# Layer 0's low weight parts on GpSimd, and a half-length Fourier transform over positions, in a two-block fp32 network

## The chip, the cores and the metric

The kernel runs on one core of a Trainium2 chip, as one launch. The metric is the device time of a launch in microseconds (us), lower is better. Six engines work side by side, each on its own queue in order: TensorE (PE, matmuls; PEld are its weight loads), VectorE (DVE), ScalarE (ACT), GpSimd (POOL), SyncE (SP, which here only issues DMAs) and 16 DMA engines that all issuers share.

## The reference, cut to what matters

Two blocks of a network in float32, on 256 tokens of width 2048. The first block has two layers (index 0 and 1); layer 0 also carries 256 context tokens, so its projections have 512 tokens and layer 1's have 256. One layer:

```python
shift, scale, gate = split(silu(c) @ ada_w[l] + ada_b[l], 3)
h = rmsnorm(x, norm_g[l]) * (1 + scale) + shift
q, k, v, up, uf, g = split_proj(h @ w_in[l])
att = attention(rope(rmsnorm(q)), [kc; rope(rmsnorm(k))], [vc; v])
mixed = concat([att, multiscale_pool(up), fourier_mix(uf)])
x = x + gate * ((mixed * silu(g)) @ w_out[l])
```

`fourier_mix` takes, for each of 4 groups of 128 channels, the real part of a two-dimensional DFT over (256 positions, 128 channels), and then a linear map:

```python
uf = u.reshape(B, N, 4, 128)
f = jnp.fft.fft2(uf, axes=(1, 3), norm='ortho').real
y = jnp.einsum('bngc,gcd->bngd', f, fourier_w)
```

The second block (gated mixing, a linear recurrence, a feed-forward part with d_ff 6144) isn't touched by the change.

## The kernel before, in words

**Weight pages.** Every large projection streams its weights in pages of 128 x 1024 floats (512 KB). `_issue` (line 91) puts the load into SP's queue, into one of 5 `wraw` buffers. `_split` (line 104) makes two fp32r tiles of it: `whi`, the rounded page, on ACT (line 259, in `split`), and `wlo`, the rest `raw - whi`, on DVE (line 260). Both have 3 buffers. `mm3` (lines 203 to 205) then does three matmuls for each product: high x high, low x high (of the activations), high x low (of the weights). `execute` (line 111) keeps up to 3 pages split ahead of the step that uses them, so a page's split can start when the page three before it has been used by the matmuls.

**Order.** The program is a list of steps. A framework orders each engine's queue by priority and by when its own plan has an instruction ready; on the chip each queue then runs strictly in that order. From `end_startup` on (`self.hot`), the two instructions of a split get high priority.

**Layer 0.** Up to about 246 us the startup works off three quarters of layer 0's first projections while the first modulation is computed. Then `end_startup` runs, and to about 827 us follow the last quarter of the first projections, the attention, pooling and Fourier branches, the four gate groups, and the output projection (`w_out`), whose last 512 columns are done in two halves of 256 tokens (pages of 24 matmuls with 256 columns). In the trace, PE uses layer 1's pages from about 827 us on; there `begin_layer1` has run.

**The modulation of later stages.** Between the weight pages, `ada_span` (line 306) streams raw pages of `ada_w` through the same 5 `wraw` buffers, in one order with the weight pages. Each raw page of layer 0's stretch is worked off by four DVE instructions of 512 columns (line 324), alternately into an accumulator `acc[0]` in SBUF and `acc[1]` in PSUM. A `wraw` buffer comes free when its last reader is done.

**The branches.** Attention, pooling and Fourier are generators that `tick` interleaves with the main steps. `fourier_tail` (line 746) does, for each group and each 256 tokens, four fp32 matmuls over channels into a `misc` bank of PSUM (three such banks), a DVE copy to `z`, then four fp32 matmuls over positions with the 128 x 2 x 256 tables `cn` and `sn` (lines 759, 760) that sum into one bank `fy`, and an ACT copy into `mixed`. There are 8 such transforms in layer 0 (4 groups x 2) and 4 in layer 1. Each fp32 matmul of the program stands as two records in the trace.

**What else is on GpSimd.** The powers of the norms (line 493), the gains of context q and k (line 599), the windows of the pooling (line 727), the running sums of squares (line 907), and DMA issues for constants and for `reload` of `xT` (line 849).

Of the kernel before, what the change touches and what calls it, by code (L numbers as in the profile page):

```python
# [11 lines left out]
ALU = mybir.AluOpType  # L12
# [4 lines left out]
P = 128  # L17
# [11 lines left out]
def f(ap):  # L29
    return ap.bitcast(F32)  # L30


class Kern:
    def __init__(self, ctx, tc, a, out):
        self.tc, self.nc, self.a, self.out = tc, tc.nc, a, out
        self.pg = ctx.enter_context(tc.tile_pool(name="pg", bufs=1))
        self.ps = ctx.enter_context(tc.tile_pool(name="ps", bufs=1, space=PSUM))
        self.dr = ctx.enter_context(tc.tile_pool(name="dr", bufs=1, space=DRAM))
        self.q_slot = 0
        self.halves = {}  # L40
        self.queue, self.active = deque(), []
        self.slot, self.start_rate, self.start_acc, self.spent = 0, 0.5, 0.0, 0.0
        self.nacc = 0
        self.late = self.hot = False


    def A(self, name, dt=F32, shape=(P, 512)):
# [56 lines left out]
    def _split(self, raw, width):  # L104
        hi = self.pg.tile([P, 1024], F32R, tag="whi", bufs=3, name="whi")
        lo = self.pg.tile([P, 1024], F32R, tag="wlo", bufs=3, name="wlo")
        with self.tc.high_priority() if self.hot else nullcontext():
            self.split(hi[:, :width], lo[:, :width], raw[:, :width])
        return hi, lo

    def execute(self, steps, ahead=3):
# [456 lines left out]
        nc.vector.scalar_tensor_tensor(lo, y[:, :256], sh, f(hi), ALU.add, ALU.subtract)  # L568

    def end_startup(self):  # L570
        self.hot = True
        self.in_order.__exit__(None, None, None)

    def spill_x(self, ks):
# [171 lines left out]
    def fourier_tail(self, gi, u, n):  # L746
        nc = self.nc
        yield 2
        for i in range(n // 256):
            zp = self.misc("fz")  # L750
            for t in range(2):
                nc.tensor.matmul(zp[:, t * 256:(t + 1) * 256], u[:, (i * 2 + t) * P:(i * 2 + t + 1) * P],
                                 self.ab[gi // 2][:, gi % 2, :], start=True, stop=True)
            z = self.S("fzs", shape=(P, 2, 256))
            nc.vector.tensor_copy(z.rearrange("p a b -> p (a b)"), zp)
            yield 3
            y = self.misc("fy")
            for t in range(2):
                nc.tensor.matmul(y[:, :256], z[:, t, 0:P], self.cn[:, t, :], start=t == 0, stop=False)
                nc.tensor.matmul(y[:, :256], z[:, t, P:2 * P], self.sn[:, t, :], start=False, stop=t == 1)  # L760
            nc.scalar.copy(self.mixed(12 + gi)[:, i * 256:(i + 1) * 256], y[:, :256])
        self.npf += 1

    def gate(self, j, src, n):
# [157 lines left out]

    def begin_layer1(self):
        self.l = 1
        self.late = True
        self.qT = {}
        self.kv_alloc()
        self.mixed = lambda j: self.xT[j][:, 256:512]
        self.h = self.pr
# [507 lines left out]
```

## Time and profile before

| | us |
|---|---|
| median of 3 runs | 2365.49 (2364.34 to 2366.28) |
| the profiled execution | 2370.99 |
| its span, first to last instruction | 2369.3 |
| busy in the span: PE / DVE / ACT / POOL | 2273.9 / 1628.4 / 1007.0 / 211.3 |

The profiled execution is 5.5 us above the median, and 1.7 us of it lie around the span. "Busy" is the time an engine's instructions took; matmul ends are modelled and overlap, so the spacing of starts, not the duration of one, is what a matmul costs in a row of them. Starts are in us from the span's start.

### The profile page before, as it was taken

How to read it: one execution, taken by the hardware profiler on the slowest of the kernel's cores; microseconds unless marked ns; L12 is line 12 of the kernel's file. 1: busy time of each engine (PE TensorE's matmuls, PEld its weight loads, DVE VectorE, ACT ScalarE, POOL GpSimd, SP SyncE). 2: the span in 40 equal slices, each digit the busy share in tenths (PEclk: the TensorE clock that was granted, in tenths of full speed). 3: DMA queues.
4: the chain of work that ended last, by engine and by line, in shares of the span. 5: the costliest groups of instructions: out<-in, count | busy, mean ns of one | idle time of the engine just before them, and what ended most of it. 6: DMA issues, size and time to landing. Idle time of an engine off the chain costs nothing.

```text
span 2369.3 us, 37423 instructions
## 1 busy us (share of the span) xinstructions
PE 2273.9 (96%) x14672; PEld 1990.0 (84%) x14672; DVE 1628.4 (69%) x2603; ACT 1007.0 (43%) x1507; POOL 211.3 (9%) x262
## 2 busy tenths in 40 slices
PE   7999898999999899999999999999999999999998
PEld 3777576877777877889998799999999999988886
DVE  4345886989888878865687966766577667664444
ACT  3322233423222455434454654554455445543433
POOL 1000203010102110010040211210000000000100
PEclk9999899999999999999999999999999999999999
DMA  9865442556766657765454554566666666765554
GB/s 328 282 233 183 144 125 60 155 179 207 238 210 207 192 156 223 249 214 183 163 180 159 159 179 162 187 189 185 186 180 186 185 181 186 218 207 187 187 187 144
DMA packets 202721, 447.89 MB, mean 189 GB/s; under 512 B 15848, under 2 KB 60288, under 8 KB 202544
## 3 DMA queue, kind: packets, MB, share of 16 engines
q1 hardware_dynamic: 193088, 428.93, 57.7%
q0 software_dynamic: 3888, 11.18, 1.4%
q10 hardware_dynamic: 5568, 5.40, 0.8%
q8 instruction: 115, 1.88, 0.3%
q14 instruction: 62, 0.51, 0.1%
HBM read 437.05 MB, written 8.39 MB: 188 GB/s over the span
## 4 chain that ended last, share of the span: by engine, by line
PE 54%; DVE 5%; issue 2%; DMA 1%; ACT 1%; POOL 1%; POOLq 0%; ACTq 0%; DVEq 0%
PE acc L205 17%; PE acc L203 17%; PE acc L204 17%; DVE wlo L260 1%; DMA wraw<-in_ada_w_dram 1%; DVE acc L324 1%; ACT whi L259 0%; DMA gw_n<-in_gm_ws_dram 0%; DVE lr L1173 0%; POOL qrs L493 0%; DMA wraw<-in_w_in_dram 0%; DVE mx L684 0%; DVE h L1001 0%; PE sc L682 0%; PE rbc L522 0%
## 5 line engine op out<-in xcount | busy, mean ns | idle before, releaser
L260 DVE TENSOR_TENSOR wlo<-wraw,whi 128x1024 fp32r<-128x1024 f32 x608 | 749.3, 1236 | 503.9 <-ACT whi L259 498.6
L259 ACT CAST whi<-wraw 128x1024 fp32r<-128x1024 f32 x608 | 636.0, 1049 | 976.9 <-PE acc L204 478.7
L203 PE MATMUL acc<-phi,whi 128*128 128x256 f32 (+1 forms) x1600 | 484.6, 303 | 14.3 <-DVE th L769 5.4
L205 PE MATMUL acc<-phi,wlo 128*128 128x256 f32 (+1 forms) x1600 | 477.8, 299 | 5.7 <-DVE wlo L260 5.7
L204 PE MATMUL acc<-plo,whi 128*128 128x256 f32 (+1 forms) x1600 | 477.4, 298 | 0.0
L203 PE MATMUL acc<-h3t,whi 128*128 128x256 f32 x1536 | 434.3, 283 | 1.3 <-DVE xT L1259 1.3
L204 PE MATMUL acc<-h3t,whi 128*128 128x256 f32 x1536 | 433.9, 283 | 0.0
L205 PE MATMUL acc<-h3t,wlo 128*128 128x256 f32 x1536 | 433.8, 282 | 0.0
L203 PEld LDWEIGHTS acc<-phi,whi 128*128 128x128 f32 x1600 | 306.6, 192 | 31.9 <-issue 9.7
L205 PEld LDWEIGHTS acc<-phi,wlo 128*128 128x128 f32 x1600 | 306.1, 191 | 17.2 <-DVE wlo L260 7.5
L324 DVE SCALAR_TENSOR_TENSOR acc<-wraw,silu_c,acc 128x512 f32<-128x512 f32 x420 | 301.3, 756 | 20.0 <-DMA wraw<-in_ada_w_dram 18.5
L204 PEld LDWEIGHTS acc<-plo,whi 128*128 128x128 f32 x1600 | 306.8, 192 | 9.2 <-issue 0.7
L203 PEld LDWEIGHTS acc<-h3t,whi 128*128 128x128 f32 x1536 | 293.3, 191 | 1.7 <-DVE xT L1259 1.7
L205 PEld LDWEIGHTS acc<-h3t,wlo 128*128 128x128 f32 x1536 | 293.4, 191 | 0.2 <-DVE wlo L260 0.2
L204 PEld LDWEIGHTS acc<-h3t,whi 128*128 128x128 f32 x1536 | 293.4, 191 | 0.0
L203 PE MATMUL acc<-hhi,whi 128*128 128x512 f32 x384 | 162.6, 424 | 5.2 <-ACT whi L259 5.2
L205 PE MATMUL acc<-hhi,wlo 128*128 128x512 f32 x384 | 154.3, 406 | 2.8 <-DVE wlo L260 2.8
L204 PE MATMUL acc<-hlo,whi 128*128 128x512 f32 x384 | 155.3, 404 | 0.0
L204 PE MATMUL acc<-wlo,act 128*128 128x512 f32 x384 | 151.7, 395 | 0.0
L203 PE MATMUL acc<-whi,act 128*128 128x512 f32 x384 | 151.7, 395 | 0.0
L205 PE MATMUL acc<-whi,act 128*128 128x512 f32 x384 | 151.7, 395 | 0.0
L203 PEld LDWEIGHTS acc<-hhi,whi 128*128 128x128 f32 x384 | 73.4, 191 | 29.0 <-ACT whi L259 7.2
(354 smaller groups left out, 2823.7 us busy)
## 6 DMA issues: line engine op xcount, KB each, us to landing
wraw<-in_w_in_dram SPq DMA_DIRECT2D x216, 512.0 KB, 3.9
wraw<-in_ffn_w_up_dram SPq DMA_DIRECT2D x192, 512.0 KB, 3.6
wraw<-in_ada_w_dram SPq DMA_DIRECT2D x128, 512.0 KB, 4.4
wraw<-in_w_out_dram SPq DMA_DIRECT2D x104, 512.0 KB, 4.4
wraw<-in_ffn_w_down_dram SPq DMA_DIRECT2D x96, 512.0 KB, 4.5
apage<-in_ada_w_dram SPq DMA_DIRECT2D x128, 256.0 KB, 5.6
xd<-xT SPq DMA_DIRECT2D x16, 256.0 KB, 3.7
xT<-xd POOLq DMA_DIRECT2D x16, 256.0 KB, 5.3
```

The source lines that it names most:

```text
L203: mm(out, lhi, rhi, start=start, stop=False)
L204: mm(out, lhi, rlo, start=False, stop=False)
L205: mm(out, llo, rhi, start=False, stop=stop)
L259: self.nc.scalar.copy(hi, src)
L260: self.nc.vector.tensor_tensor(lo, src, f(hi), ALU.subtract)
L324: nc.vector.scalar_tensor_tensor(acc[m], x, cm, acc[m], ALU.mult, ALU.add)
```

## The change

Two edits. First, `wlo` of a weight page is computed by GpSimd instead of DVE for the pages that are split between `end_startup` and `begin_layer1`; the rounded part stays on ACT. Second, the transform over positions computes its cosine and sine parts for positions 0 to 128 only, in two column ranges of one bank; ACT copies the sine part to SBUF, and DVE writes the sum for positions 0 to 128 and the difference, read backwards, for positions 129 to 255.

```diff
@@ class Kern, __init__
-        self.late = self.hot = False
+        self.late = self.hot = self.wide = False
@@ _split
         with self.tc.high_priority() if self.hot else nullcontext():
-            self.split(hi[:, :width], lo[:, :width], raw[:, :width])
+            self.nc.scalar.copy(hi[:, :width], raw[:, :width])
+            eng = self.nc.gpsimd if self.wide else self.nc.vector
+            eng.tensor_tensor(lo[:, :width], raw[:, :width], f(hi[:, :width]), ALU.subtract)
@@ end_startup
-        self.hot = True
+        self.hot = self.wide = True
@@ fourier_tail
             y = self.misc("fy")
-            for t in range(2):
-                nc.tensor.matmul(y[:, :256], z[:, t, 0:P], self.cn[:, t, :], start=t == 0, stop=False)
-                nc.tensor.matmul(y[:, :256], z[:, t, P:2 * P], self.sn[:, t, :], start=False, stop=t == 1)
-            nc.scalar.copy(self.mixed(12 + gi)[:, i * 256:(i + 1) * 256], y[:, :256])
+            for x, (tab, o) in enumerate(((self.cn, 0), (self.sn, P))):
+                for t in range(2):
+                    nc.tensor.matmul(y[:, x * 256:x * 256 + 129], z[:, t, o:o + P], tab[:, t, 0:129], start=t == 0,
+                                     stop=t == 1)
+            q = z[:, 0, 0:129]
+            nc.scalar.copy(q, y[:, 256:385])
+            m = self.mixed(12 + gi)[:, i * 256:(i + 1) * 256]
+            nc.vector.tensor_tensor(m[:, 0:129], y[:, 0:129], q, ALU.add)
+            nc.vector.tensor_tensor(m[:, 129:256], y[:, 127:0:-1], q[:, 127:0:-1], ALU.subtract)
@@ begin_layer1
-        self.late = True
+        self.late, self.wide = True, False
```

## Rows read from the trace of the kernel before

**Rows 1.** By stage: us, busy us of PE, PEld, DVE, ACT, POOL, PEclk, DMA, GB/s

```profile
246.00:440.00 194.00, 175.67 (x825) 136.94 (x825) 156.81 (x323) 66.06 (x137) 36.82 (x56) 0.95 0.37 108
440.00:607.00 167.00, 165.85 (x787) 130.50 (x785) 148.19 (x249) 55.71 (x95) 12.70 (x25) 1.00 0.61 189
607.00:760.00 153.00, 142.58 (x612) 110.28 (x613) 132.75 (x201) 37.73 (x49) 16.80 (x17) 0.97 0.67 212
760.00:827.00 67.00, 59.06 (x433) 55.38 (x432) 55.31 (x88) 29.06 (x42) 10.52 (x9) 0.92 0.62 200
```

**Rows 2.** Waits of PE from 246 to 827 us: total, times, longest

```profile
PE acc L203 <- ACT whi L259: 9.0, 3, 5.2
PE pTp L694 <- DVE p L690: 6.3, 3, 3.4
PE acc L203 <- DVE th L769: 5.4, 2, 4.5
PE acc L205 <- DVE wlo L260: 4.3, 3, 2.8
PE acc L203 <- DVE xT L855: 3.5, 4, 1.4
```

**Rows 3.** Waits of SP's queue, the page loads, 246 to 827 us

```profile
SPq L101 <- DVE wlo L260: 180.0, 63, 21.7
SPq L101 <- DVE acc L324: 167.9, 81, 5.6
```

**Rows 4.** Groups by line, DVE, 246 to 827 us: busy, mean ns, idle before

```profile
L324 DVE SCALAR_TENSOR_TENSOR acc<-wraw,silu_c,acc 128x512 f32<-128x512 f32 x351 | 249.7, 756 | 5.4 <-DMA wraw<-in_ada_w_dram 4.5
L260 DVE TENSOR_TENSOR wlo<-wraw,whi 128x1024 fp32r<-128x1024 f32 x83 | 104.4, 1257 | 44.5 <-ACT whi L259 41.4 <-PE poolmm L737 1.8 <-PE acc L204 0.9
```

**Rows 5.** Chain that ended last, 985 to 1062 us: start, us, what

```profile
997.81 2.68 PE pv L700 x24
...
1037.72 1.73 PE fz L752 x8
...
1044.64 0.43 PE fy L759 x2
```

**Rows 6.** Tile fy: count, ns min/median/max, first and last start

```profile
L759 PE MATMUL fy<-cn,fzs x48: 377/379/379, 324.4 to 1058.7; 128*128 128x256 f32 x48
L761 ACT COPY mix<-fy x8: 372/372/373, 326.3 to 354.8; 128x256 f32<-128x256 f32 x8
```

**Rows 7.** By 20 us, around layer 0's Fourier branch, columns as in Rows 1

```profile
320.00:340.00 20.00, 20.00 (x95) 16.95 (x94) 19.59 (x46) 3.02 (x10) 4.09 (x9) 1.00 0.54 158
340.00:360.00 20.00, 19.65 (x89) 14.67 (x88) 9.94 (x20) 8.06 (x16) 0.00 (x0) 1.00 0.19 53
```

**Rows 8.** Tile mix: DVE copies out of PSUM, 128 columns

```profile
L702 DVE COPY mix<-pv x32: 270/290/292, 312.9 to 484.2; 128x128 f32<-128x128 f32 x32
```

**Rows 9.** Tiles sq and x2r: GpSimd's two-input instructions, 256 and 512 columns

```profile
L907 POOL TENSOR_TENSOR sq<-sq,sqt x45: 727/932/1721, 1180.0 to 1544.9; 128x256 f32<-128x256 f32 x45
L1347 POOL TENSOR_TENSOR x2r<-x2r,fg x6: 1290/1578/2272, 2225.2 to 2296.4; 128x512 f32<-128x512 f32 x6
```

**Rows 10.** Order of time, POOL and DVE at 283 us: start, us, instruction

```profile
283.30 1.64 POOL L599 TENSOR_TENSOR qq<-qq,gb_q 128x512 f32<-128x512 f32 x1 [0.87 <-DVE qq L597]
...
283.73 2.28 DVE L260 TENSOR_TENSOR wlo<-wraw,whi 128x1024 fp32r<-128x1024 f32 x1
```

**Rows 11.** Tile plo, DVE: beside GpSimd's sums (h) and without them (yn)

```profile
L260 DVE TENSOR_TENSOR plo<-h,phi x16: 409/948/961, 1180.4 to 1253.9; 128x256 fp32r<-128x256 f32 x16
L260 DVE TENSOR_TENSOR plo<-yn,phi x16: 416/418/421, 1404.2 to 1459.8; 128x256 fp32r<-128x256 f32 x16
```

**Rows 12.** Groups by line, POOL, 246 to 827 us

```profile
L493 POOL TENSOR_TENSOR qrs<-qrs,nhalf 128x4 f32<-128x4 f32 (+1 forms) x12 | 12.3, 1025 | 79.3 <-DVE qrs L492 79.3
```

**Rows 13.** Order of time, PE at 1037 us: matmuls of 256 columns in a row

```profile
1037.20 0.28 PE L203 MATMUL acc<-phi,whi 128*128 128x256 f32 x1
1037.32 0.28 PE L204 MATMUL acc<-plo,whi 128*128 128x256 f32 x1
```

## The prediction, made before the change was run

> **What bounds the kernel now.** I read the page's busy shares first: PE is busy in 2273.9 of 2369.3 us, so whatever is changed can only pay through the matmuls it removes or through the time in which PE stands still. Next came the table by stage. In the stretch that the first edit touches, 246 to 827 us, PE is idle for 18.3 + 1.2 + 10.4 + 7.9 = 37.8 of 581 us, and DVE is busy in 493.1 of them [rows 1]. The reader is to see two engines near their limit at once: PE first, DVE close behind. Then the waits of PE in this stretch. Those that name DVE are 6.3 (p), 5.4 (th), 4.3 (wlo) and 3.5 (xT), 19.5 us together, and 9.0 us name `whi` on ACT [rows 2]. ACT is no slow engine here; what makes `whi` late is the page, and SP's queue shows why: its page loads waited 180.0 us on DVE's `wlo` and 167.9 us on DVE's line 324, the readers that give `wraw` buffers back [rows 3]. So 28.5 us of PE's idle time go back to DVE. DVE itself loses 44.5 us standing at the head of its queue with a `wlo` whose `whi` isn't there yet, while the raw pages' work waits behind it [rows 4]. After 827 us only the second edit counts; there the chain of waits runs through PE, the Fourier matmuls of layer 1 among its links [rows 5].
>
> **The Fourier transform.** The four matmuls of a transform are 8 records, 96 in all (48 for `cn` [rows 6], and as many for `sn`). Records of 256 columns follow one another at 1.73/8 = 0.216 us (the two of `fy` in 0.43 us agree), records of 128 columns at 2.68/24 = 0.112 us [rows 5]. 129 columns I price as 128. The gain is 96 x (0.216 - 0.112) = 10.0 us of PE: 64 records, 6.7 us, in layer 0 and 32 records, 3.3 us, in layer 1. Layer 1's part lies on the chain and counts in full. Layer 0's records lie between 324 and 355 us [rows 6], where PE is busy in 39.65 of 40 us [rows 7], so PE is the limit there too, unless the evacuation takes its place.
>
> The evacuation grows: before, one ACT copy of 0.37 us [rows 6]; after, a copy of half the columns (between 0.2 and 0.37, I take 0.3) and then two DVE instructions, which I price by DVE's 128-column copy out of PSUM, 0.29 us [rows 8]. The bank `fy` is held some 0.5 us longer, plus DVE's queue, where up to two instructions of 0.756 us [rows 4] can stand ahead. With three `misc` banks and two used per transform, the next `fz` or `fy` may wait. The trace shows no such wait before; from below it costs nothing, from above it eats layer 0's 6.7 us. DVE is full from 320 to 340 us and half empty from 340 to 360 [rows 7], so I take 1.5 us. Edit two: -10.0 + 1.5 = -8.5 us, between -10.3 (the columns' ratio) and -3.3.
>
> **The low parts, what DVE loses and GpSimd gets.** DVE drops the 83 `wlo` of the stretch, 104.4 us, and the 44.5 us it stood before them [rows 4], or 1.26 + 0.54 = 1.80 us per page. GpSimd gets 83 instructions of 1024 columns. None stands in the trace. Its fastest of 256 and of 512 columns took 0.727 and 1.290 us [rows 9], so 0.563 more per 256 columns, and 1.290 + 2 x 0.563 = 2.42 us for 1024; from above, twice the median of 512 columns, 3.16 us. I take 2.42, since the medians hold waits that I count apart. That is 201 us in 581 on an engine that was busy in 76.8 [rows 1]: room on the average. ACT's part of a split doesn't change.
>
> The trace shows that the two engines don't run such instructions side by side. At 283 us a `wlo` of DVE, begun 0.43 us after a GpSimd product of 1.64 us, took 2.28 us in place of some 1.2: about as much more as the product still had to run [rows 10]. Beside GpSimd's sums, DVE's `plo` took 948 ns in the median, and 418 without them, about one sum more [rows 11]. So a GpSimd instruction with two inputs shuts out DVE's instructions with two SBUF inputs until it ends, and the other way round. [...]
>
> How long is DVE shut out per page? Call it b, between 0 and the hold, 2.42. DVE's main work, line 324, alternates between the accumulator in SBUF (two SBUF inputs, shut out) and the one in PSUM (free to run, 0.756 us). If GpSimd starts while DVE always has work, then half a free instruction or a whole one still passes, and DVE stands for the rest: b = 2.42 - 0.38 = 2.04 if the lock is taken during a free instruction, 2.42 - 0.756 = 1.66 if it is taken right after a shut-out one, 1.85 in the mean. But DVE was without work for 88 of 581 us [rows 1], and in the attention much of its work reads PSUM. I take b = 1.5. DVE's other work is (493.1 - 104.4)/83 = 4.68 us per page, the stretch 7.00 us per page: 6.48 before, 6.18 after. DVE is relieved by 0.3 us per page, 25 us in the stretch, and no more, although 104 us of work leave it. PE gets a part: of its 28.5 us I take a third, -9.5; the wait on `wlo` and half of that on `whi` go, the evacuations stay.
>
> **What the edit costs.** (1) The last 16 pages of `w_out` are used in 24 x 0.12 = 2.9 us each [rows 13]. GpSimd needs 2.42 for each, waits for DVE's instruction in progress (0.25 in the mean) and has 8 sums of 0.73 [rows 9] to do in between: 16 x 2.67 + 5.8 = 48.5 against 46.1 us. I take +3, between 0 and +8. (2) The 12 powers of the norms [rows 12] now stand in one queue with instructions of 2.42 us, and behind each power the attention's q or k waits, with DVE in front of it. Splits hold GpSimd for 201/581 = 0.35 of the time, so the delay is 0.35 x 1.2 = 0.4 us for each, 5 us, more if a split waits for a load in front of a power; +2.5, between 0 and +10. (3) The DMA issues of `reload` stand in the same queue and wait for the end of the gates; a split behind them would start late, one time. It is in the bounds of (1).
>
> Edit one: -9.5 + 3 + 2.5 = -4 us, between -28.5 and, at b = 2.42, (2.42 - 1.80) x 83 = +51.
>
> **Sum.** -8.5 - 4 = -12.5 us: 2371.0 to 2358.5 against the profiled execution, and from the median of the runs 2365.5 to 2353.
>
> **Rivals.**
> *The shared lock makes DVE slower.* Mechanism: GpSimd's hold of 2.42 us against the 1.80 us that DVE spent per page. For: in the steady parts DVE always has line 324 waiting, and there b is 1.85, above 1.80. Against: DVE's idle time. At b = 2.1 DVE needs 0.3 us more per page, and as page loads wait on DVE [rows 3], that comes out at the end: +25 - 8.5 = +16.5, 2382. It decides from b = 1.80 + 8.5/83 = 1.90 on. Chance 0.25. [...]
> *GpSimd frees DVE fully.* All 28.5 us come back and none of the costs shows: -37, 2328. For: the 44.5 us at the head of DVE's queue. Against: rows 10 and 11. Chance 0.10.
> *Nothing to see.* Layer 0's Fourier gain turns into waits for banks, and edit one comes out even: -3.3, 2362. Chance 0.16.
> *GpSimd writes fp32r slowly.* No row shows GpSimd writing that type. At twice the price, 4.84 us, a page's DVE time is 4.68 + 4.3 = 9.0 against 7.00: +165 us, 2520. Against it: DVE's `wlo` of 1024 columns (1257 ns) costs less per column than its f32 work of 512 (756 ns), so there the type isn't paid for [rows 4]. Chance 0.04.
> *The forecast* has the remaining 0.45; its own range is 2343 to 2360.
>
> **Numbers.** This kernel's measurement can tell about 0.2%, 4.7 us, from no change. Faster: 0.45 + 0.10 = 0.55. Same: 0.16. Slower: 0.25 + 0.04 = 0.29. The range 2334 to 2384 leaves out the slow write (0.04), half of the full relief (0.05) and the lock at b above 2.13 (0.10).
>
> **What the profile after would show.** Fourier: records of some 0.11 us, 96 of them, and no new wait of PE on ACT's copy or DVE's sums there. GpSimd: 83 to 85 `wlo` near 2.4 us or longer, and none before 246 us. Lock: line 324 in layer 0 with a longer mean than 756 ns; (mean - 0.756) x 351 is 83 b, so 0.36 us more at b = 1.5. If it is 0.43 or more, the first rival holds. PE's idle time between end of startup and layer 1 tells the rest: under 30 us the forecast is right, at 38 or more edit one gave nothing. The prediction is wrong if GpSimd's instruction takes clearly more than 3 us, if its order puts splits behind powers or loads that wait, or if PE starts waiting on `wlo` by more than the 4.3 us of before.

## The result, and the profile after

The changed kernel takes 2394.77 us in the median of 4 runs (2391.31 to 2398.10), against 2365.89 for the kernel before, run beside it: a ratio of 1.0121, interval 1.0099 to 1.0143, so some 29 us slower. The prediction was 2353, and its range ended at 2384. The profiled execution took 2391.46 us, its span 2389.7.

First the table by stage of the changed kernel; it answers to [rows 1] and has its columns.

```profile
246.00:440.00 194.00, 168.79 (x813) 131.90 (x813) 158.76 (x322) 63.70 (x135) 76.16 (x73) 0.94 0.37 112
440.00:607.00 167.00, 157.95 (x742) 123.96 (x741) 143.31 (x214) 53.23 (x92) 63.44 (x37) 0.98 0.54 166
607.00:760.00 153.00, 138.33 (x602) 108.76 (x601) 132.51 (x169) 37.58 (x50) 75.81 (x50) 0.94 0.65 212
760.00:827.00 67.00, 56.40 (x362) 49.67 (x361) 49.88 (x66) 22.46 (x29) 45.32 (x23) 0.92 0.66 211
```

PE is idle for 59.5 of 581 us where it was idle for 37.8, and its granted clock is lower in three of four stages. The time is lost in this stretch: layer 1's first use of a page moves from 827.0 to 846.3 us and the span grows by 20.4, nearly as much. DVE's busy time is 484.5 us where it was 493.1, but by 827 us less of the work is done. Counted to layer 1's first page, over the same work, it rose to 501.5, although 104.4 us of low parts had left DVE.

Next the waits of PE in the stretch, as [rows 2]; then those of SP's queue, as [rows 3]. Line numbers are those of the changed kernel, so L205 is here the first matmul of `mm3`, which was L203.

```profile
PE acc L205 <- DVE xT L863: 13.9, 2, 8.0
PE acc L205 <- DVE th L777: 13.5, 4, 8.8
PE sc L684 <- ACT qT L674: 7.3, 2, 6.6
PE pTp L696 <- DVE p L692: 7.1, 4, 2.9
PE acc L205 <- ACT whi L108: 6.0, 1, 6.0
...
PE acc L207 <- POOL wlo L110: 2.2, 2, 1.4
```

```profile
SPq L101 <- POOL wlo L110: 241.5, 57, 22.0
SPq L101 <- DVE acc L326: 191.3, 72, 8.3
```

The wait on `wlo` has shrunk, as forecast, but the waits on evacuations of PSUM banks (`th`, `xT`) went from 8.9 to 27.4 us, and that on the query chain (`qT`) from 0.7 to 7.3. Groups by line, DVE and then POOL, same stretch, as [rows 4]:

```profile
L326 DVE SCALAR_TENSOR_TENSOR acc<-wraw,silu_c,acc 128x512 f32<-128x512 f32 x350 | 305.0, 919 | 22.2 <-DMA wraw<-in_ada_w_dram 21.1
L692 DVE TENSOR_SCALAR p<-p,rc 128x512 f32<-128x512 f32 (+1 forms) x32 | 19.5, 611 | 0.5
```

```profile
L110 POOL TENSOR_TENSOR wlo<-wraw,whi 128x1024 fp32r<-128x1024 f32 x77 | 190.7, 2479 | 235.7 <-ACT whi L108 184.8 <-PE pv L702 21.9 <-PE poolmm L739 8.8
```

GpSimd's instruction costs 2.48 us, near the 2.42 forecast. The raw pages' instruction (line 326, line 324 before) went from 756 to 919 ns. Two places show how. In order of time, DVE (first fence) and POOL (second): start, duration.

```profile
401.06 2.87 DVE L599 TENSOR_TENSOR qq<-qq,qrs 128x512 f32<-128x512 f32 x1
...
408.68 5.96 DVE L326 SCALAR_TENSOR_TENSOR acc<-wraw,silu_c,acc 128x512 f32<-128x512 f32 x5
...
617.24 13.51 DVE L326 SCALAR_TENSOR_TENSOR acc<-wraw,silu_c,acc 128x512 f32<-128x512 f32 x15
630.67 0.68 DVE L777 SCALAR_TENSOR_TENSOR th<-th,acc 128x512 f32<-128x512 f32 x1
```

```profile
400.95 2.44 POOL L110 TENSOR_TENSOR wlo<-wraw,whi 128x1024 fp32r<-128x1024 f32 x1
...
411.05 2.36 POOL L110 TENSOR_TENSOR wlo<-wraw,whi 128x1024 fp32r<-128x1024 f32 x1
```

The scaling of q at 401.06 takes 0.69 us where it took 2.87 here: GpSimd began 0.11 us earlier, and DVE came through when it ended. The query chain runs through this instruction, and PE then waits 6.6 us for `qT`. At 617 us, 15 raw-page instructions stand in front of the evacuation for which PE waits 8.8 us. So long a run is new: with the low parts gone from DVE's queue, up to 46 raw-page instructions follow one another in it, where the longest run before was 9. What such a wait costs beyond itself is in the windows of 4 us around it, columns as above:

```profile
620.00:624.00 4.00, 2.58 (x12) 1.73 (x10) 4.00 (x7) 2.03 (x3) 1.87 (x1) 1.00 0.45 137
624.00:628.00 4.00, 0.00 (x0) 0.00 (x0) 4.00 (x5) 0.00 (x0) 0.92 (x1) 0.87 0.80 262
628.00:632.00 4.00, 0.60 (x2) 0.50 (x3) 4.00 (x8) 0.00 (x0) 0.00 (x0) 0.50 0.68 158
632.00:636.00 4.00, 4.00 (x11) 3.13 (x10) 4.00 (x7) 3.06 (x5) 1.23 (x1) 0.50 0.87 303
```

After PE has stood still here, its granted clock is 0.50 from 628 to 636 us, and 11 matmuls pass in 4 us where 19 or 20 passed before.

The Fourier part, tile `fy` of the changed kernel, as [rows 6]:

```profile
L763 PE MATMUL fy<-cn,fzs x48: 272/275/276, 321.4 to 1077.2; 128*128 128x129 f32 x48
...
L766 ACT COPY fzs<-fy x12: 267/268/270, 322.6 to 1078.0; 128x129 f32<-128x129 f32 x12
L768 DVE TENSOR_TENSOR mix<-fy,fzs x8: 279/285/295, 323.5 to 351.5; 128x129 f32<-128x129 f32 x8
```

### The profile page after: what moved, and what is told of

Read it like the earlier page. It is cut to its first block, busy times and chain, and to the rows that moved or that the text cites. A ratio compares the mean times of both kernels' runs of the same rounds, so it can differ in the third digit from the quotient of the medians.

```text
span 2389.7 us, 37443 instructions
## 1 busy us (share of the span) xinstructions
PE 2267.7 (95%) x14672; PEld 1988.2 (83%) x14672; DVE 1639.6 (69%) x2542; ACT 1006.0 (42%) x1507; POOL 417.8 (17%) x347
## 4 chain that ended last, share of the span: by engine, by line
PE 63%; DVE 15%; issue 5%; DMA 3%; POOL 2%; ACT 1%; POOLq 0%; ACTq 0%; DVEq 0%
PE acc L205 20%; PE acc L206 20%; PE acc L207 20%; DVE acc L326 6%; DMA wraw<-in_ada_w_dram 2%; DVE wlo L110 1%; DMA wraw<-in_w_in_dram 1%; PE sc L684 1%; PE pv L702 1%; ACT whi L108 1%; DVE plo L570 1%; DVE lr L1181 1%; DVE plo L262 1%; POOL wlo L110 1%; POOL sqa L915 1%
## 5 line engine op out<-in xcount | busy, mean ns | idle before, releaser
L110 DVE TENSOR_TENSOR wlo<-wraw,whi 128x1024 fp32r<-128x1024 f32 x523 | 643.5, 1235 | 459.2 <-ACT whi L108 456.8
L205 PE MATMUL acc<-phi,whi 128*128 128x256 f32 (+1 forms) x1600 | 484.6, 303 | 23.9 <-DVE xT L863 13.9
L205 PE MATMUL acc<-h3t,whi 128*128 128x256 f32 x1536 | 434.4, 283 | 1.3 <-DVE xT L1267 1.3
L326 DVE SCALAR_TENSOR_TENSOR acc<-wraw,silu_c,acc 128x512 f32<-128x512 f32 x420 | 358.4, 895 | 35.2 <-DMA wraw<-in_ada_w_dram 33.4
L205 PEld LDWEIGHTS acc<-phi,whi 128*128 128x128 f32 x1600 | 306.8, 192 | 40.0 <-issue 19.5
L205 PEld LDWEIGHTS acc<-h3t,whi 128*128 128x128 f32 x1536 | 293.4, 191 | 1.7 <-DVE xT L1267 1.7
L110 POOL TENSOR_TENSOR wlo<-wraw,whi 128x1024 fp32r<-128x1024 f32 x85 | 210.0, 2474 | 443.2 <-ACT whi L108 392.2
L205 PE MATMUL acc<-hhi,whi 128*128 128x512 f32 x384 | 164.7, 429 | 10.7 <-ACT whi L108 6.0
L205 PE MATMUL acc<-whi,act 128*128 128x512 f32 x384 | 151.7, 395 | 0.0
```

The lines of the kernel that those rows point to most:

```text
L110: eng.tensor_tensor(lo[:, :width], raw[:, :width], f(hi[:, :width]), ALU.subtract)
L205: mm(out, lhi, rhi, start=start, stop=False)
L326: nc.vector.scalar_tensor_tensor(acc[m], x, cm, acc[m], ALU.mult, ALU.add)
```

## The experiments

Lines differ by a few between the kernels; names are the same. Differences in us are differences of ratios to the kernel before, times its 2366 to 2370 us.

**Which edit.** Each alone: `self.hot = True` in place of `self.hot = self.wide = True` leaves the Fourier edit; the kernel before with the edits of `_split`, `end_startup` and `begin_layer1` is the other.

> The Fourier edit alone, low parts left on DVE. The prediction's sum for it is -8.5 us (-10.3 to -3.3), so about 2357. Theory 1 (the whole loss of the two edits together, +29 us, belongs to the low parts): 2353 to 2363. Rival (the shorter transform also re-orders the queues behind it and loses): above 2368. Layer 1's part, 32 records shorter by 0.104 us, should show as about 3 us less between the start of layer 1 and h3t; in the kernel with both edits that stretch came out 0.8 us longer, so a figure near 0 says that layer 1's gain is hidden by something else.

> GpSimd's low parts alone, the transform as before. Theory 1 (all of the loss comes from this edit): 2398 to 2405, that is the kernel with both edits plus what the Fourier edit gains. If instead the two edits work against each other only together: below 2385. In either case PE should wait on the bank evacuations (th, xT) for 20 us or more between 240 and 860 us where it waited 9 us before.

The Fourier edit alone: 2355.76 us (2348.98 to 2359.10), ratio 0.9951, interval 0.9932 to 0.9970: -11.6 us. GpSimd alone: 2400.00, ratio 1.0132, interval 1.0117 to 1.0147. The whole loss is the low parts'; between the Fourier edit alone and both edits lie 0.0170, 40 us. With GpSimd alone PE waits 26.7 us on `th` and `xT`, more than the 20 expected. The Fourier edit's table by stage:

```profile
246.00:440.00 194.00, 177.45 (x877) 139.39 (x877) 166.17 (x356) 68.48 (x144) 36.09 (x56) 0.96 0.37 112
440.00:607.00 167.00, 163.30 (x768) 127.25 (x767) 149.37 (x246) 54.86 (x92) 13.67 (x26) 1.00 0.63 203
607.00:760.00 153.00, 142.96 (x645) 110.27 (x644) 134.37 (x204) 39.71 (x52) 19.19 (x18) 1.00 0.65 208
760.00:827.00 67.00, 59.62 (x424) 55.40 (x422) 58.35 (x92) 31.91 (x48) 11.15 (x11) 0.95 0.62 199
```

To see where the loss lies, the two kernels are compared over the same work, from 246 us to layer 1's first use of a page (first line: the Fourier edit alone; second: both edits; columns as above):

```profile
246.00:814.10 568.10, 531.91 (x2658) 423.35 (x2657) 497.30 (x877) 187.41 (x323) 76.13 (x106) 0.98 0.55 173
246.00:846.30 600.30, 539.13 (x2663) 431.74 (x2663) 501.52 (x793) 186.91 (x323) 274.52 (x188) 0.95 0.52 164
```

Both edits need 32.2 us more for it: PE is idle for 61.2 us against 36.2, 25.0 more, and busy for 7.2 more with the same matmuls, at a lower granted clock (0.95 for 0.98). The idle time is thus the larger part by far. Another 7 us are lost in the first 25 us of layer 1: there PE waits 1.9 us on GpSimd's last low part and 2.9 us on its sums `sqa` (1.5 in the Fourier edit alone), and the granted clock falls once more, to 0.50 from 854 to 862 us. The two profiled executions differ by 42 us in all, but the one of the Fourier edit alone is 7 us faster than its median, so these parts are good to a few us. The growth of the delay is seen in the starts of the high parts on ACT (the count of the page from 233 us on, then its start):

```
page   Fourier alone   both edits   difference
  12          351.57       355.07          3.5
  30          511.43       533.04         21.6
  45          607.28       633.66         26.4
  75          783.91       813.78         29.9
  90          831.73       870.98         39.2
```

**Is it the order of DVE's queue?**

```diff
-        nc.vector.scalar_tensor_tensor(t[:, :n], t[:, :n], 1.0, src, ALU.add, ALU.mult)
+        with self.tc.high_priority() if self.wide else nullcontext():
+            nc.vector.scalar_tensor_tensor(t[:, :n], t[:, :n], 1.0, src, ALU.add, ALU.mult)
```

and the same around the evacuation in `resid`.

> Both edits, and the DVE instruction that empties a gate's bank (the first of the two) and the one that empties an output bank of layer 0 get high priority, so that the order no longer puts raw-page work of the same time ahead of them. Theory order (DVE has more than enough time, but its queue, written by a plan that knows no lock, has runs of up to 15 raw-page instructions ahead of an evacuation, 13.5 us): the waits on th and xT, 27 us, mostly go, 2365 to 2378. Theory lock (DVE is late because GpSimd's instructions stretch its own, wherever they stand): the waits move to other tiles, p, plo, whi, and the time stays above 2385.

2391.30 us, ratio 1.0098, interval 1.0076 to 1.0121: no gain that the measurement tells from both edits. The waits on `th` (13.4 us) and `xT` (13.7) stayed, and the 15 raw-page instructions still stood ahead of the evacuation, so the edit did not change the order where it mattered. It shows only that this priority is no cure. What the order is worth is seen below, in a kernel that has the same order without the subtraction.

**Does it cost because of what GpSimd's instruction is?** The low part as one copy, then as two, on GpSimd's pages only. Both kernels leave out the subtraction, so the low part is not the rest any more.

```diff
-            eng.tensor_tensor(lo[:, :width], raw[:, :width], f(hi[:, :width]), ALU.subtract)
+            eng.tensor_copy(lo[:, :width], raw[:, :width])
+            eng.tensor_copy(lo[:, :width], f(hi[:, :width]))   # second run only
```

> Both edits, but GpSimd makes the low part by a copy of the raw page: one input in place of two. The subtraction of the high part is left out, and with it the wait for ACT's high part. Theory lock: if a one-input instruction of GpSimd shuts DVE out less, or takes less time, the mean of DVE's raw-page instruction falls from 917 ns towards 756 and the time falls to about 2370. Theory order: the mean may fall, but the time stays above 2385 as long as DVE's queue has runs of raw-page work ahead of evacuations.

> Both edits, but GpSimd writes the low part's tile twice by one-input copies, first of the raw page, then of the high part (the subtraction is left out; the tile holds the high part in the end). Each copy took 1.125 us, so a page holds GpSimd 2.25 us, nearly the 2.42 of the subtraction, and it reads the same two tiles and waits for the same two engines. Theory lock (what costs is that GpSimd's two-input instruction shuts DVE out): 2325 to 2345, and DVE's raw-page instruction stays near 780 ns. Rival occupancy (what costs is that low parts come out of GpSimd late and that the norms' powers and q's products queue behind them there): 2375 to 2395, though 780 ns.

One copy: 2328.47 us, ratio 0.9833 (0.9816 to 0.9849). Two copies: 2344.02, ratio 0.9893 (0.9874 to 0.9912). With nearly the same time on GpSimd the loss is gone. But SP's loads then waited mostly for ACT's high part, 215 us between 246 and 860, and hardly for GpSimd, 33: with the raw page read first, its buffer comes free earlier. That was a second difference which the expectation had missed; it is taken up below.

**Where.** GpSimd's share switched on, or off, at the `flush` ahead of the third gate group:

```diff
             if g == 0:
                 main += flush
+                main.append(([], lambda: setattr(self, "wide", True)))   # or False
```

> Both edits, but GpSimd takes the low parts only from the third gate group on (about 55 of 85 pages; the attention's stretch stays with DVE as before). Against the kernel with the Fourier edit alone the one with both loses 21.6 us up to page 30 (520 us) and 17 us after it, by the starts of the high parts. Theory place-bound (each stretch loses for itself): 2356 + 17 = 2373. Theory attention only (the delay of the attention's chain sets the whole loss, the gates and the output lose only because they start in a bad phase): 2352 to 2362.

> The counterpart: both edits, GpSimd takes the low parts only up to the third gate group (some 30 pages, those beside the attention). Theory place-bound: 2356 + 21 = 2377. Theory gates only: 2352 to 2362.

Late: 2377.05 us, ratio 1.0034 (1.0021 to 1.0048), 19.7 us above the Fourier edit alone. Early: 2381.79, ratio 1.0051 (1.0032 to 1.0071), 23.7 us above. The two make 43, both edits 40: each stretch loses for itself, with 56 pages and with 29.

**Shorter holds.**

```diff
+            n = 256 if self.wide else width
+            for o in range(0, width, n):
+                eng.tensor_tensor(lo[:, o:o + n], raw[:, o:o + n], f(hi[:, o:o + n]), ALU.subtract)
```

> Both edits, GpSimd's subtraction in four pieces of 256 columns. The fastest such instruction took 0.727 us, so a page holds GpSimd 2.9 us in place of 2.4, but never more than 0.73 at a stretch. Theory latency (what costs is that single short instructions of DVE, on which PE waits, stand up to 2.4 us): faster than with one piece, 2375 to 2388. Theory throughput (what costs is the sum of the time that DVE is shut out): slower, 0.5 us x 83 pages at most, 2400 to 2435.

2381.90 us, ratio 1.0048 (1.0028 to 1.0068): 17 us faster than one piece, though GpSimd is busy longer. Lines of DVE and POOL in this run (240 to 860 us, and the whole span):

```profile
L328 DVE SCALAR_TENSOR_TENSOR acc<-wraw,silu_c,acc 128x512 f32<-128x512 f32 x354 | 280.8, 840 | 40.5 <-DMA wraw<-in_ada_w_dram 39.2
```

```profile
L112 POOL TENSOR_TENSOR wlo<-wraw,whi 128x256 fp32r<-128x256 f32 x340 | 281.9, 860 | 383.5 <-ACT whi L108 360.2 <-PE pv L704 15.1 <-PE poolmm L741 7.2
```

**Is DVE short of time?** The accumulator in SBUF is dropped from the raw pages' work:

```diff
-                for m in range(nm):
+                for m in range(nm - 1, nm):
```

> The Fourier edit alone with half of the raw pages' work: only the accumulator in PSUM is kept, the one in SBUF is left out (its sum is taken from the other). DVE loses some 178 x 0.75 = 133 us of 493 between 246 and 827 us and is no limit any more. It is the control for the next run: 2310 to 2345.

> Both edits with half of the raw pages' work left out in the same way, so that DVE has time to spare and nearly all raw-page work left reads one operand from PSUM. Theory sum (GpSimd's hold costs because DVE's time in the stretch is short): the loss against the control is gone, -8 to +5 us. Theory chain (the hold costs because it falls on the few DVE instructions on which PE waits at once, in the attention above all): 10 to 20 us of the 39 remain.

Fourier edit alone: 2325.01 us, ratio 0.9816 (0.9801 to 0.9831). Both edits: 2357.93, ratio 0.9956 (0.9939 to 0.9972). 33 us of the loss remain, more than either theory had, with DVE busy in only 335.5 of 581 us. The sum of DVE's time is not what costs. PE still waited 6.3 us for `th`; DVE in order of time there:

```profile
611.45 1.54 DVE L326 SCALAR_TENSOR_TENSOR acc<-wraw,silu_c,acc 128x512 f32<-128x512 f32 x2 [3.78 <-DMA wraw<-in_ada_w_dram]
612.90 0.68 DVE L777 SCALAR_TENSOR_TENSOR th<-th,acc 128x512 f32<-128x512 f32 x1
```

An idle DVE stood at the head of its queue with a raw page that hadn't landed. This made a second theory: GpSimd holds a page's load buffer longer, and so the next raw page is late.

**Shut out, or buffers held?** The two copies in the other order (high part first, so that the raw page stays held to the end); and, without GpSimd, the high part written twice by ACT.

```diff
+            if self.hot and not self.late:
+                self.nc.scalar.copy(hi[:, :width], raw[:, :width])
```

> Both edits, GpSimd writes the low part's tile by two one-input copies as before, but first from the high part and then from the raw page (the subtraction is left out). So the page's load buffer stays held until GpSimd's second copy ends, 2.3 us after the high part, as with the subtraction; in the run with the raw page first it came free with the high part. Theory lock (a two-input instruction of GpSimd shuts DVE out): 2340 to 2355, like the other order of the copies. Theory buffer (a page's load buffer comes free later, so the next raw page lands later, and DVE's queue stands at its head with the evacuations behind): 2375 to 2395.

> The Fourier edit alone, low parts on DVE, but ACT writes each high part of this stretch twice, so that the low part starts 1.05 us later and the page's load buffer is held 1.05 us longer, about the 1.2 us that GpSimd's subtraction takes longer than DVE's, with no instruction of GpSimd added. Theory lock: little, 2356 to 2366. Theory buffer: most of the 39 us that separate the kernel with both edits from this one, 2375 to 2395.

> Both edits with the accumulator in SBUF left out of the raw pages' work, and GpSimd's two one-input copies, the high part first, in place of its subtraction (left out). DVE has time to spare, as in the pair of runs with half of the raw pages' work, which stood at 2325 (Fourier edit) and 2358 (both edits). Theory lock on the chain: the 33 us between those two are the two-input instruction's too, so 2315 to 2335. If a late low part or the longer held buffer makes them, 2345 to 2360.

High part first: 2349.21 us, ratio 0.9911 (0.9892 to 0.9930). High part twice: 2355.52, ratio 0.9932 (0.9911 to 0.9953). The buffer theory falls. From the start of its high part to the last read of its raw page, a page's load buffer is held 3.9 us in the mean under the subtraction, 3.8 in each of these two kernels, and 2.5 in the Fourier edit alone; the longer hold alone costs nothing that shows. With half of the raw pages' work the two copies give 2336.08, ratio 0.9863 (0.9844 to 0.9883), 1 us above what the shut-out theory expected: of the 33 us, 22 belong to the subtraction as against the copies, and 11 remain with GpSimd's work as such. The run with the high part first, DVE (246 to 827 us) and POOL (whole span):

```profile
L330 DVE SCALAR_TENSOR_TENSOR acc<-wraw,silu_c,acc 128x512 f32<-128x512 f32 x350 | 263.0, 798 | 31.4 <-DMA wraw<-in_ada_w_dram 30.4
```

```profile
L112 POOL CAST wlo<-wraw 128x1024 fp32r<-128x1024 f32 x85 | 102.9, 1210 | 4.7
L111 POOL CAST wlo<-whi 128x1024 fp32r<-128x1024 f32 x85 | 95.3, 1121 | 434.7 <-ACT whi L108 389.1 <-PE pv L706 17.6 <-PE poolmm L743 17.5
```

The order of DVE's queue falls as a cause by itself, too. This kernel has the runs of raw-page instructions that the changed kernel has, 46 long at the most, and the same 15 stand in front of the same evacuation; in order of time, DVE:

```profile
593.30 10.49 DVE L330 SCALAR_TENSOR_TENSOR acc<-wraw,silu_c,acc 128x512 f32<-128x512 f32 x15
603.72 0.67 DVE L781 SCALAR_TENSOR_TENSOR th<-th,acc 128x512 f32<-128x512 f32 x1
```

They take 10.49 us where they took 13.51, and PE waits 1.7 us on `th` and 5.8 on `xT` in the whole stretch, in place of 13.5 and 13.9. Whether the subtraction would cost as much under the old order was not run.

GpSimd is held 2.33 us per page, nearly as long as by the subtraction, but the raw pages' instruction is stretched by 41 ns (798 for 757 in the Fourier edit alone) and not by 162. The copies can shut DVE out, though; from the same run, in order of time:

```profile
566.07 1.15 DVE L266 TENSOR_TENSOR plo<-mix,phi 128x512 fp32r<-128x512 f32 x1
```

```profile
565.63 1.04 POOL L111 CAST wlo<-whi 128x1024 fp32r<-128x1024 f32 x1 [3.05 <-ACT whi L108]
...
566.74 1.38 POOL L112 CAST wlo<-wraw 128x1024 fp32r<-128x1024 f32 x1
```

DVE's product took 1.15 us in place of 0.68, as if it had begun when the first copy ended, and the second copy took 1.38 in place of 1.04, begun while DVE's product ran. So it is not only a two-input instruction of GpSimd that shuts DVE out, as the expectations had it. That the copies cost less because DVE gets a turn between them fits these rows, but is argued, not shown.

**Candidates.** Pieces only from the last gate group to the third group of the output projection; and, on the Fourier edit alone, `nc.scalar.activation(p, p, AF.Copy, scale=rc)` for the normalisation of p.

> The Fourier edit, and GpSimd's low parts in pieces of 256 columns only from the last gate group to the third group of the output projection (36 pages), where the kernel with pieces throughout lost nothing against the Fourier edit alone. A candidate for a version faster than the Fourier edit alone: 2346 to 2358 if that stretch has a gain of its own, above 2360 if GpSimd loses there too.

> The Fourier edit alone, and the attention's normalisation of p on ACT in place of DVE (32 instructions, 12 to 13 us of DVE; ACT is busy in a third of the stretch). PE waits 6.1 us on p between 300 and 540 us. If DVE's place in that chain is what PE waits for, 2346 to 2353; if the chain only moves to ACT's queue, 2353 to 2360.

2352.55 us, ratio 0.9934 (0.9919 to 0.9949), and 2361.65, ratio 0.9971 (0.9958 to 0.9983), above the range expected. The first is level with the Fourier edit alone, whose interval it overlaps; both are faster than the kernel before and the changed one. Moving p gains nothing; where that chain waits then was not followed.

## Why the prediction was wrong, point by point

**Fourier, -8.5: right.** 96 records with 129 columns, four in 0.445 us in a row of them, 0.111 each against the 0.112 priced; no new wait of PE but 0.4 us on `fzs`. Alone the edit gave -11.6 us, interval -16.1 to -7.1. The division into 6.7 us for layer 0 and 3.3 for layer 1 is not borne out by the traces, nor refuted: from layer 1's first page to the second block's first matmul on `h3t` the Fourier edit alone took 9.4 us less than the kernel before, both edits 1.2 more, so the executions vary by more than the 3.3.

**GpSimd's price, 2.42: right** (2.48 in the mean). The slow write of fp32r didn't happen. The first low part on GpSimd starts at 234.9 us, not after 246: the order had drawn some splits forward.

**How long DVE is shut out, b = 1.5: too much, and the wrong test.** By the prediction's own formula, (0.919 - 0.756) x 351 / 83, it is 0.69 us per page on the raw pages. That is below the 1.90 from which the first rival was to decide, so by its test the forecast should have held. But the formula looks at the raw pages alone. Over all of DVE's instructions, an estimate is (501.5 - 493.1 + 104.4 - 4.5)/85 = 1.3 us per page, with 4.5 for the two new Fourier instructions: still below 1.5, so b isn't what made the forecast wrong. The other sign was clear: at 38 us or more of PE's idle time the edit was to have given nothing, and it is 59.5. (Of the readings for the lock, "about one sum more" is 530 ns against sums of 727 at the least, so most of a sum.)

**The step that failed: "DVE is relieved by 0.3 us per page ... PE gets a part: of its 28.5 us I take a third, -9.5".** It weighed the shut-out as a sum of DVE time that PE shares in. The runs show that this sum isn't what PE feels: with DVE busy in 58% of the stretch, 33 of 40 us are lost all the same. A hold of 2.4 us can fall on an instruction that heads DVE's queue, as on the scaling of q (2.87 us for 0.69), and everything behind it, the evacuations too, comes later. The relief itself rested on the 0.54 us per page for which DVE had stood before `wlo`, since 1.26 us of work less 1.5 of shut-out gives none; that time didn't come free, as DVE is idle for 98.8 us up to layer 1's first page where it was for 87.9. In place of -9.5 the term, with costs (1) and (2), was +40 by the runs. In the traces, up to layer 1's first page, it is 25 us of PE's idle time and 7 of longer matmuls at a lower granted clock. The prediction had no term for the clock, though [rows 1] show it, nor for the new order of DVE's queue.

**"The evacuations stay"** failed with it: `th` and `xT` went from 8.9 to 27.4 us.

**Cost (1), the last 16 pages, +3 (0 to +8): wrong sign for the pages themselves.** On PE they take 53.2 us with both edits, against 61.6 in the kernel before and 59.7 in the Fourier edit alone. But they begin behind PE's wait of 8.0 us on `xT`, which may have let their pages get ready; with it they take 61.2. The 0.25 us of waiting for DVE in this cost were an estimate that no row stands behind; in the trace the mean of GpSimd's subtractions, 2.48, is 0.14 above their shortest, 2.34. The table of starts, where both edits lose 9.3 us from page 75 to 90, counts when a page is split and not when PE needs it, and reaches into layer 1. **Cost (2), the powers, +2.5 (0 to +10):** the wait on `qT`, 7.3 us, is where they stand, but the part of a power in it isn't separated from the shut-out of line 599.

**The rival that came true** is the first, the shared lock, by its mechanism and sign; its price of 2382 was 13 us short and its condition, b above 1.90 as a price of DVE's time per page, was not met and is not the one that decides. The trace shows the hold by the 2.87 us at 401.06, in place of 0.69, beside a subtraction of 2.44 begun 0.11 us earlier.

**What stays open:** what the subtraction would cost without the long runs of raw-page instructions; why two copies stretch the raw pages' instruction a quarter as much as one subtraction of nearly the same total length (41 ns against 162), while four pieces of a subtraction stretch it half as much (840 ns); what the 11 us are that remain beside the copies, of which a part may be the new order of DVE's queue; and how the losses divide among the chains.

## What to carry to other kernels

Where two engines shut each other out, price the hold as a delay of whichever instruction it shuts out on a queue that PE waits for (here 2.87 us for 0.69), not as a share of the slower engine's time; a spare engine of half the speed, here 2.48 us a page for 1.26, can then cost more than it frees. Cut what must go there into short instructions: pieces of 0.86 us in the mean gave back 17 of the 40 us. When work leaves a queue, look at the new order of what is left: runs that it used to break grow long, here from 9 to 46, and an evacuation behind such a run feels the holds in it: 15 instructions took 13.51 us with the subtraction, 10.49 with the copies. Add what a lower granted TensorE clock costs: here 7 us, at 0.95 for 0.98, beside 25 of idle time. And compare kernels over the same work: in the same 581 us DVE seems relieved by 9 us, over the same work its busy time grew by 8.

## What the runs showed of the hardware

A DVE instruction with one SBUF input can be shut out as well: the normalisation of p, one input and an output in SBUF, went from 415 to 611 ns in the mean, and at 420.23 us it took 2.53 beside a subtraction of 2.37 begun at 420.11. Not all are: in the run of both edits with the accumulator in PSUM alone, a raw pages' instruction took 0.76 us at 616.90 beside a subtraction of 2.39 begun at 616.47, and 0.75 at 621.74 with none beside it. A one-input copy of 1024 columns on GpSimd shut DVE out too: in the rows at 565.63 us DVE's product took 1.15 for 0.68 beside a copy of 1.04, and held up the next copy in turn, 1.38 for 1.04. Two-input sums are held up as well: in the kernel before, a GpSimd sum that took 0.73 us at the least took 1.36 at 1183.95, beside a `wlo` of DVE begun at 1183.51. ACT wrote every high part twice, 79 us more of ACT in the stretch, at no cost that shows (ratio 0.9932 against 0.9951).
